# A conformer trunk: one chunk's taps moved between two projection halves, and layer norm's steps in another written order

## The chip, the cores and the metric

The kernel runs on one core of one Trainium2 chip. The metric is the device time of one execution, in microseconds. A core has five engines that run beside each other, each with a queue of its own that is worked off strictly in order: TensorE (PE, matmuls; its weight loads are listed as PEld), VectorE (DVE), ScalarE (ACT), GpSimd (POOL) and SyncE (SP), which here only starts DMAs. They wait for each other by semaphores. Matmul results land in PSUM, everything else lies in SBUF; the inputs and two small scratch tensors lie in DRAM.

## The reference

Two layers of a decoder on a sequence of 512 positions and 1024 channels. The change lies in the first one's mixer, a causal convolution module; the differential attention of the second layer, the two SwiGLU blocks and the gated embeddings are untouched.

```python
def conformer_conv(x, w_pw1, b_pw1, dw_w, dw_b, ln_g, ln_b, w_pw2, b_pw2):
    a = x @ w_pw1 + b_pw1
    u = a[..., :D_MODEL] * jax.nn.sigmoid(a[..., D_MODEL:])
    u = lax.conv_general_dilated(
        u, dw_w[:, None, :].astype(u.dtype), window_strides=(1,),
        padding=[(CONV_WIDTH - 1, 0)],
        dimension_numbers=("NWC", "WIO", "NWC"),
        feature_group_count=D_MODEL) + dw_b
    u = jax.nn.silu(layer_norm(u, ln_g, ln_b))
    return u @ w_pw2 + b_pw2

def reference(...):
    ...
    h = x
    for i in range(DEPTH):
        ...
            u = rms_norm(h, conv_norm_g[j])
            h = h + conformer_conv(u, conv_w_pw1[j], ...)
        ...
        u = rms_norm(h, ffn_norm_g[i])
        h = h + swiglu(u, ffn_w_gate[i], ffn_w_up[i], ffn_w_down[i])
        gate = jax.nn.sigmoid(rms_norm(h, ple_norm_g[i]) @ ple_w_gate[i])
        h = h + gate * (p[i] @ ple_w_proj[i])
    return h
```

The convolution has 31 taps and works on each channel alone; layer norm runs over the 1024 channels of a position.

## The kernel before

**Layout.** Activations are held transposed: eight chunks of 128 channels (on the partitions) by 512 positions. A float32 product is made of three matmuls on operands split into a rounded high part and the low rest (`mm3`, lines 165 to 169: low weight by high input, high by high, high by low). The weights are split on the chip: `weight` (line 148) loads 512 KB into `wraw`, ACT casts the high part `whi` (line 160), and VectorE subtracts it for the low part `wlo` (line 162).

**The convolution.** The loop over chunks c = 0 to 7 (line 549) makes two halves of the first projection for each chunk, gate and value, 24 matmuls each (`half`), multiplies them by the norm's row (L583, L589) and gates them (L595 or L603). The taps are spread over engines. Chunks 1, 3, 5 and 6 are "phased": all taps run on TensorE as 72 small matmuls (L457). For that, the gated chunk goes to DRAM (`pi<-big`, L420) and comes back regrouped in four pieces (`C<-pi`, L424), and nine tap matrices of 256 KB are loaded by SP (`D<-in_diag` and `C<-in_diag`, L437 to L447), four of them into buffers that the taps of an earlier phased chunk give free. The result is copied out of PSUM by ACT (L465), written to DRAM on ACT's own queue (`po<-big`, L467), read back by SP in four pieces (`B<-po`, L470), and VectorE adds bias and a shift (L475). That makes the chunk's output `y[c]`. Chunk 7, the last, is shared by three engines: VectorE makes one part as a chain of scaled additions (L505, L508), ACT and POOL a second (L495, L496), and TensorE the third, eight taps, behind all halves (L413). L512 and L514 add the three.

The table `BETWEEN` and `BEHIND` (lines 62 and 63) says behind which half of which chunk a phased chunk's taps are issued: `BETWEEN[c]` between the halves of chunk c, `BEHIND[c]` behind both. Chunk 5's taps stand behind chunk 6's halves, chunk 6's behind chunk 7's.

**Statistics.** For each finished chunk ACT makes the square (L536), and POOL adds the sum of squares and of values (L541, L543); for chunk 6 VectorE does these two. The five products of the layer's embedding factors (`factor`, `project`: six matmuls and a copy by ACT, L375) fill TensorE while chunk 7's sum is made; a sixth and two more follow later.

**Layer norm.** Behind chunk 7's sum, TensorE turns the sums into columns (L198), VectorE makes the variance in four small steps (L647, L648, L649, L259), POOL takes the power -1/2 (L261), ACT multiplies the identity by the four columns (L657), and TensorE spreads the result to a row (L660, tile `lrow`). Meanwhile TensorE makes the mean's row (L642, L643). VectorE centres chunks 0 to 2 by it (L654), POOL chunks 3 to 7 (L665). Then for each chunk: VectorE multiplies by `lrow` (L671), ACT applies Silu with gain and bias (L672) and casts the high part (L674), VectorE subtracts for the low part (L676). These are z, the input of the second projection (`linear`, line 682), whose first group makes three output chunks at a time.

**What sets the order.** The program is written in one order, and a scheduler places each engine's instructions by simulated times, except where `manual_schedule` keeps the written order on the engines named, or `issue_after` holds an instruction behind another. Buffers rotate by tag; whoever writes one waits for its last reader.

## Time and profile before

| | |
|---|---|
| median of 3 runs | 1249.22 us (1247.81 to 1250.43) |
| the profiled execution | 1246.65 us, of which the span 1244.8 us |
| mean granted clock of TensorE | 0.999 |
| chain that ended last | PE 84%, DVE 7%, issue 4%, ACT 2%, POOL 2%, DMA 1% |
| the changed stretch | about 95 to 172 us |

The span reaches from the first to the last recorded instruction. In a timeline a row gives start, duration, engine, source line, operation, output and inputs by the program's names, shape and count; in brackets stands how long the engine had been idle before it, and what ended that. A table of waits gives engine, line and releaser, with the total, the number of waits and the longest. A table of windows gives for a stretch its length, the busy time of PE, PEld, DVE, ACT and POOL with their instruction counts, the granted clock of TensorE, the busy share of the DMA engines and GB/s.

### The profile page before, as it was taken

Reading aid. Unit: us, or ns where it says so; the run is one execution under the profiler, and the core shown is the slowest. Engines: PE = TensorE matmul, PEld = TensorE weight load, DVE = VectorE, ACT = ScalarE, POOL = GpSimd, SP = SyncE. Lnnn points to the kernel's source line nnn. Section 1 sums busy time; section 2 is a strip of 40 time slices with the busy share of each in tenths; the row PEclk is TensorE's granted clock in tenths of the full one; section 3 lists DMA queues with packets and bytes.
Section 4 is the critical chain, followed back from the end, with each engine's and each line's share of the span. In section 5 each row is a group of like instructions: output and inputs, shape, how many; then the busy total and the mean of one; then the engine's idle time right before and its main releaser. Section 6 shows DMA issues by size and latency. Waiting matters only on the chain.

```text
span 1244.8 us, 18364 instructions
## 1 busy us (share of the span) xinstructions
PE 1231.8 (99%) x7048; PEld 1078.6 (87%) x7048; DVE 879.8 (71%) x1244; ACT 623.7 (50%) x1098; POOL 464.7 (37%) x351
## 2 busy tenths in 40 slices
PE   9999999999999999999999999999999999999998
PEld 7887788888998899888888888788889998999887
DVE  5997866985895479547676876646966885588535
ACT  7742464433553255435666877735434552455432
POOL 0953442024670464133436645041026650552120
PEclk9999999999999999999999999999999999999999
DMA  9756214234233322334332331142233333232331
GB/s 328 226 179 189 82 54 121 92 98 127 88 100 118 102 86 78 109 104 153 130 116 63 112 94 34 52 150 87 90 127 90 103 113 111 83 102 86 105 98 68
DMA packets 50019, 138.44 MB, mean 111 GB/s; under 512 B 5731, under 2 KB 10851, under 8 KB 49932
## 3 DMA queue, kind: packets, MB, share of 16 engines
q1 hardware_dynamic: 47664, 133.71, 34.1%
q10 hardware_dynamic: 2268, 3.57, 1.0%
q8 instruction: 55, 0.90, 0.3%
q14 instruction: 32, 0.26, 0.1%
HBM read 130.94 MB, written 6.31 MB: 110 GB/s over the span
## 4 chain that ended last, share of the span: by engine, by line
PE 84%; DVE 7%; issue 4%; ACT 2%; POOL 2%; DMA 1%; SPq 0%; DVEq 0%; POOLq 0%; ACTq 0%
PE mm L167 26%; PE mm L168 25%; PE mm L169 25%; DVE wlo L782 2%; POOL wk L496 1%; PE mm L1188 1%; DVE sc L508 1%; DVE wlo L162 1%; PE sc L457 1%; PE sc L1155 1%; PE sc L1156 1%; DVE B L873 1%; PE mm L457 1%; PE tp L1175 1%; PE tp L1109 1%
## 5 line engine op out<-in xcount | busy, mean ns | idle before, releaser
L160 ACT CAST whi<-wraw 128x1024 fp32r<-128x1024 f32 (+1 forms) x139 | 141.2, 1024 | 219.8 <-PE mm L169 110.3
L162 DVE TENSOR_TENSOR wlo<-wraw,whi 128x1024 fp32r<-128x1024 f32 (+1 forms) x135 | 174.2, 1296 | 81.9 <-ACT whi L160 81.1
L167 PE MATMUL mm<-A,wlo 128*128 128x512 f32 (+1 forms) x552 | 214.0, 388 | 0.1
L168 PE MATMUL mm<-A,whi 128*128 128x512 f32 (+1 forms) x552 | 213.4, 387 | 0.0
L169 PE MATMUL mm<-A,whi 128*128 128x512 f32 (+1 forms) x552 | 211.0, 388 | 0.0
L167 PE MATMUL mm<-B,wlo 128*128 128x512 f32 x352 | 137.0, 389 | 0.0
L168 PE MATMUL mm<-B,whi 128*128 128x512 f32 x352 | 137.0, 389 | 0.0
L169 PE MATMUL mm<-B,whi 128*128 128x512 f32 x352 | 135.6, 389 | 0.0
L228 POOL TENSOR_TENSOR acc<-acc,wk 128x512 f32<-128x512 f32 x35 | 60.3, 1724 | 189.8 <-ACT wk L227 189.2
L168 PE MATMUL mm<-C,whi 128*128 128x256 f32 x448 | 126.8, 283 | 0.0
L167 PE MATMUL mm<-C,wlo 128*128 128x256 f32 x448 | 126.8, 283 | 0.0
L169 PE MATMUL mm<-C,whi 128*128 128x256 f32 x448 | 126.8, 283 | 0.0
L169 PEld LDWEIGHTS mm<-A,whi 128*128 128x128 f32 x552 | 103.6, 188 | 22.3 <-DVE A L206 1.1
L167 PEld LDWEIGHTS mm<-A,wlo 128*128 128x128 f32 x552 | 103.8, 188 | 21.7 <-DVE h L1319 0.5
L168 PEld LDWEIGHTS mm<-A,whi 128*128 128x128 f32 x552 | 103.8, 188 | 20.5
L782 DVE TENSOR_TENSOR wlo<-A,whi 128x1024 fp32r<-128x1024 f32 x60 | 107.5, 1802 | 19.7 <-ACT whi L781 19.7
L781 ACT CAST whi<-A 128x1024 fp32r<-128x1024 f32 x60 | 62.9, 1048 | 54.6 <-PE mm L169 43.8
L791 POOL TENSOR_TENSOR A<-wraw 128x512 f32<-128x512 f32 x16 | 23.7, 1482 | 169.8 <-DMA wraw<-in_wts 147.0
L791 POOL TENSOR_TENSOR A<-A 128x512 f32<-128x512 f32 x16 | 24.6, 1536 | 165.3 <-DMA A<-in_wts 162.6
L168 PEld LDWEIGHTS mm<-C,whi 128*128 128x128 f32 x448 | 86.0, 192 | 0.2
L167 PEld LDWEIGHTS mm<-C,wlo 128*128 128x128 f32 x448 | 86.0, 192 | 0.2
L169 PEld LDWEIGHTS mm<-C,whi 128*128 128x128 f32 x448 | 86.0, 192 | 0.0
(324 smaller groups left out, 3057.1 us busy)
## 6 DMA issues: line engine op xcount, KB each, us to landing
wraw<-in_wts SPq DMA_DIRECT2D x159, 512.0 KB, 3.6
A<-in_wts SPq DMA_DIRECT2D x32, 512.0 KB, 3.6
wraw<-in_wts SPq DMA_DIRECT2D x16, 384.0 KB, 3.1
D<-in_diag SPq DMA_DIRECT2D x22, 256.0 KB, 4.5
C<-in_diag SPq DMA_DIRECT2D x16, 256.0 KB, 4.7
h<-in_xT SPq DMA_DIRECT2D x8, 256.0 KB, 4.7
B<-in_xtok SPq DMA_DIRECT2D x4, 512.0 KB, 7.2
rest<-h SPq DMA_DIRECT2D x8, 256.0 KB, 2.6
```

The costliest lines, as they stand in the source:

```text
L160: A.copy(hi[:, cut], raw[:, cut])
L162: eng.tensor_tensor(lo[:, cut], raw[:, cut], f(hi[:, cut]), ALU.subtract)
L167: T.matmul(acc, al, bh, start=first, stop=False, **kw)
L168: T.matmul(acc, ah, bh, start=False, stop=False, **kw)
L169: return T.matmul(acc, ah, bl, start=False, stop=last, **kw)
L228: self.last = self.eng.tensor_tensor(self.acc, self.acc, sq, ALU.add)
L457: last_tap[0] = T.matmul(acc[:, g * P : (g + 1) * P], w, ups[c][:, g, LEAD - m : LEAD - m + P], start=(m == 0), stop=(m == LAGS - 1),)
L496: G.tensor_tensor(pacc, pacc, pr, ALU.add)
L508: last_v_tap[0] = V.scalar_tensor_tensor(sum_, tap(j), wt(c, j), sum_, ALU.mult, ALU.add)
L781: A.copy(hi, src)
L782: V.tensor_tensor(lo, src, f(hi), ALU.subtract)
L791: G.tensor_tensor(s[:, 0], r1[:, 0], r1[:, 1], ALU.add)
```

## The change

Four things are edited.

1. Chunk 5's taps move from `BEHIND[6]` to `BETWEEN[7]`. The hold in chunk 7's chain of scaled additions behind chunk 6's shift moves from the fourth tap from the end on to the last alone.
2. The sixth factor's matmuls are written out, and its copy by ACT is written behind the four diagonal pieces.
3. Three weights of the second projection are made ahead of the variance; the third one's low part is now written ahead of the four small steps on VectorE, which are kept in that order.
4. Layer norm's steps on VectorE and ACT stand in a written order: for chunks 0 to 2, centring and product of the next chunk alternate, and a second Silu writes the high part straight from the product, in place of the cast. Chunks 3 to 7 keep Silu and cast. The first group's matmul order on chunks 0 and 1 is written out.

```diff
-BETWEEN = ((), (0,), (), (1, 2), (), (3, 4), (), ())
-BEHIND = ((), (), (), (), (), (), (5,), (6,))
+BETWEEN = ((), (0,), (), (1, 2), (), (3, 4), (), (5,))
+BEHIND = ((), (), (), (), (), (), (), (6,))
...
-            with tc.issue_after(last_shift[0].ins) if alone and j == KW - 4 else nullcontext():
+            with tc.issue_after(last_shift[0].ins) if alone and j == KW - 1 else nullcontext():
...
+        if acc is not None:
+            A.copy(o, acc)
+            pp.append(o)
+            return
...
-    factor(last_moment)
+    fifth = mm()
+    for k in range(2):
+        with tc.issue_after(last_moment[0].ins):
+            last_product[0] = mm3(fifth, wpart(pw[1], 2 + k), ph[k], k == 0, k == 1)
...
-    V.tensor_scalar(vs[:, 4:8], first_of(sums["mcols"]), 1.0 / D, None, ALU.mult)
-    V.tensor_tensor(vs[:, 4:8], vs[:, 4:8], vs[:, 4:8], ALU.mult)
-    V.scalar_tensor_tensor(vs[:, 0:4], first_of(sums["cols"]), 1.0 / D, vs[:, 4:8], ALU.mult, ALU.subtract)
-    r = rsqrt_cols(vs[:, 0:4], 4, 1.0)
-    layer_v = last_v[0]
-    with tc.issue_after(layer_v.ins):
-        for c in range(3):
-            V.scalar_tensor_tensor(y[c], sums["mean"], -1.0 / D, y[c], ALU.mult, ALU.add)
-    dg = wk()
-    for b in range(4):
-        last_dg = A.activation(dg[:, b * P : (b + 1) * P], ident, AF.Copy, scale=r[:, b : b + 1])
-    lrow = tp()
-    with tc.issue_after(last_product[0].ins):
-        last_product[0] = T.matmul(lrow, ones, dg, start=True, stop=True)
-    drow = wk()
-    with tc.issue_after(last_dg.ins):
-        A.mul(drow, sums["mean"], -1.0 / D)
-    for c in range(3, NC):
-        G.tensor_tensor(y[c], y[c], drow, ALU.add)
+    outer = [weight(after=(last_add[0], None)) for _ in range(2)]
+    raw = sb([P, 1024], "C5", 2)
+    outer.append((sb([P, 1024], "whi", 4, F32R), sb([P, 1024], "wlo", 4, F32R)))
+    nc.sync.dma_start(raw, wts[wnext[0]])
+    wnext[0] += 1
+    A.copy(outer[2][0], raw)
+    with tc.manual_schedule(engines={V.engine}):
+        V.tensor_tensor(outer[2][1], raw, f(outer[2][0]), ALU.subtract)
+        V.tensor_scalar(vs[:, 4:8], first_of(sums["mcols"]), 1.0 / D, None, ALU.mult)
+        V.tensor_tensor(vs[:, 4:8], vs[:, 4:8], vs[:, 4:8], ALU.mult)
+        V.scalar_tensor_tensor(vs[:, 0:4], first_of(sums["cols"]), 1.0 / D, vs[:, 4:8], ALU.mult, ALU.subtract)
+        r = rsqrt_cols(vs[:, 0:4], 4, 1.0)
+    dg, drow, lrow = wk(), wk(), tp()
...
+    def silu(out, c):
+        return A.activation(out, y[c], AF.Silu, scale=col("ln_g", c), bias=col("ln_b", c))
...
     with tc.manual_schedule(engines={V.engine, A.engine}):
-        for c in range(NC + 2):
-            if c < NC:
-                V.tensor_tensor(y[c], y[c], lrow, ALU.mult)
-                A.activation(y[c], y[c], AF.Silu, scale=col("ln_g", c), bias=col("ln_b", c))
+        for b in range(4):
+            A.activation(dg[:, b * P : (b + 1) * P], ident, AF.Copy, scale=r[:, b : b + 1])
+        factor(None, fifth)
+        with tc.issue_after(last_product[0].ins):
+            last_product[0] = T.matmul(lrow, ones, dg, start=True, stop=True)
+        centre(0)
+        A.mul(drow, sums["mean"], -1.0 / D)
+        for c in range(3, NC):
+            G.tensor_tensor(y[c], y[c], drow, ALU.add)
+        scaled_by_row(0)
+        for c in range(3):
+            if c < 2:
+                centre(c + 1)
+                scaled_by_row(c + 1)
+            z.append(both(sb([P, 2, S], f"A{c}", 1, F32R)))
+            silu(z[c][0], c)
+            silu(y[c], c)
+            if c < 2:
+                factor(last_product)
+            if c > 0:
+                rest(c - 1)
+        for c in range(3, NC + 1):
+            if c < NC:
+                scaled_by_row(c)
+                silu(y[c], c)
                 z.append(both(sb([P, 2, S], f"A{c}", 1, F32R)))
                 hi = A.copy(z[c][0], y[c])
-            if c >= 2:
-                lo = V.tensor_tensor(z[c - 2][1], y[c - 2], f(z[c - 2][0]), ALU.subtract)
-            if c < 2:
-                factor(last_product)
+            lo = rest(c - 1)
             if c == 3:
                 third = lo, hi
```

`centre`, `scaled_by_row` and `rest` are the three VectorE steps of before (centring, product, low part), each as a function of the chunk.

TensorE, where chunk 7's gate half and chunk 5's taps meet. Names: `mm_1085` (before) and `mm_1022` (now) are the gate half of chunk 7, `mm_1110` and `mm_1100` its value half, `sc` is chunk 5's tap sum. Before:

```order
L169 MATMUL mm_978<-A_40_172,whi_749 128x512
L167 MATMUL mm_1085<-A_33_141,wlo_943 128x512
L168 MATMUL mm_1085<-A_33_141,whi_942 128x512
L169 MATMUL mm_1085<-A_33_141,whi_942 128x512
L167 MATMUL mm_1085<-A_34_146,wlo_943 128x512
L168 MATMUL mm_1085<-A_34_146,whi_942 128x512
L457 MATMUL sc_1003<-C_162_867,D_187_1004 128x128 x4
```

And of the change:

```order
L167 MATMUL mm_1022<-A_40_172,wlo_943 128x512
L168 MATMUL mm_1022<-A_40_172,whi_942 128x512
L169 MATMUL mm_1022<-A_40_172,whi_942 128x512
L457 MATMUL sc_1047<-C_162_867,D_193_1048 128x128 x4
L457 MATMUL sc_1047<-C_162_867,D_194_1050 128x128 x4
```

Before, the taps stood behind five of the gate half's 24 matmuls; now they stand behind all 24.

ACT between chunk 7's halves and the tap products. `big<-sc` with the DMA `po` is chunk 5's way out, `wk_1223` chunk 5's square, `whi_1453` (before) and `whi_1367` (now) the high part of a later weight, whose buffer chunk 7's value half frees. Before:

```order
L160 CAST whi_1218<-wraw_1217 128x1024
L465 COPY big_1071<-sc_1003 128x512
L467 DMA po_1073<-big_1071 128x512
L536 ACTIVATE wk_1207<-B_176_915 128x512
L160 CAST whi_1447<-wraw_1446 128x1024
L584 ACTIVATE big_1188<-big_1188,vec_63 128x512
```

And of the change:

```order
L536 ACTIVATE wk_1207<-B_176_915 128x512
L160 CAST whi_1367<-wraw_1366 128x1024
L465 COPY big_1187<-sc_1047 128x512
L495 ACTIVATE C_238_1287<-C_211_1184,C_31_133 128x512
L467 DMA po_1189<-big_1187 128x512
L495 ACTIVATE C_239_1290<-C_211_1184,C_31_133 128x512
L495 ACTIVATE C_240_1293<-C_211_1184,C_31_133 128x512
L495 ACTIVATE C_241_1296<-C_211_1184,C_31_133 128x512
L536 ACTIVATE wk_1223<-B_213_1191 128x512
L465 COPY big_1197<-mm_1125 128x512
```

Chunk 5's copy and DMA now stand behind the cast and the first tap product, and chunk 5's square stands ahead of chunk 6's copy. On VectorE chunk 5's shift (L475) moves accordingly from ahead of chunk 7's gating to behind the sixth step of chunk 7's chain, and chunk 6's shift from four steps ahead of its end to two. On SP chunk 6's regrouped input now leaves ahead of all of its first four tap matrices, and chunk 5's return behind both matrices of chunk 7.

VectorE from the end of the convolution into layer norm. `B_244` is chunk 7's output, `v` the variance's columns, `B_82`, `B_117`, `B_129` chunks 0 to 2, `A` the low parts of z. Before:

```order
L514 TENSOR_TENSOR B_244_1305<-mm_1227,B_244_1305 128x512
L162 TENSOR_TENSOR wlo_1448<-wraw_1446,whi_1447 128x1024
L162 TENSOR_TENSOR wlo_1454<-wraw_1452,whi_1453 128x1024
L647 TENSOR_SCALAR v_253_1361<-sc_1333 128x4
L648 TENSOR_TENSOR v_253_1361<-v_253_1361 128x4
L649 SCALAR_TENSOR_TENSOR v_253_1361<-tp_1331,v_253_1361 128x4
L259 TENSOR_SCALAR v_254_1365<-v_253_1361 128x4
L162 TENSOR_TENSOR wlo_1460<-C_276_1458,whi_1459 128x1024
L654 SCALAR_TENSOR_TENSOR B_82_376<-tp_1332,B_82_376 128x512
L654 SCALAR_TENSOR_TENSOR B_117_609<-tp_1332,B_117_609 128x512
```

And of the change:

```order
L162 TENSOR_TENSOR wlo_1368<-wraw_1366,whi_1367 128x1024
L661 TENSOR_TENSOR wlo_1374<-C_259_1372,whi_1373 128x1024
L662 TENSOR_SCALAR v_252_1359<-sc_1333 128x4
L663 TENSOR_TENSOR v_252_1359<-v_252_1359 128x4
L664 SCALAR_TENSOR_TENSOR v_252_1359<-tp_1331,v_252_1359 128x4
L259 TENSOR_SCALAR v_262_1383<-v_252_1359 128x4
L669 SCALAR_TENSOR_TENSOR B_82_376<-tp_1332,B_82_376 128x512
L672 TENSOR_TENSOR B_82_376<-B_82_376,tp_1390 128x512
L669 SCALAR_TENSOR_TENSOR B_117_609<-tp_1332,B_117_609 128x512
L672 TENSOR_TENSOR B_117_609<-B_117_609,tp_1390 128x512
L669 SCALAR_TENSOR_TENSOR B_129_647<-tp_1332,B_129_647 128x512
L680 TENSOR_TENSOR A_268_1410<-B_82_376,A_268_1410 128x512
```

The third weight's low part moved from behind the variance's steps to ahead of them. Two of the three centrings moved behind a product with the row `tp_1390`, and the first low part of z behind all three products.

More of the change, by code (lines that the diff above doesn't have):

```diff
@@ L612, in trunk, with factor @@
     pw = [weight(), weight()]
-    def factor(after):
+    def factor(after, acc=None):
         m = len(pp)
@@ L655, in trunk @@
-    dg = wk()
-    for b in range(4):
-        last_dg = A.activation(dg[:, b * P : (b + 1) * P], ident, AF.Copy, scale=r[:, b : b + 1])
-    lrow = tp()
-    with tc.issue_after(last_product[0].ins):
-        last_product[0] = T.matmul(lrow, ones, dg, start=True, stop=True)
-    drow = wk()
-    with tc.issue_after(last_dg.ins):
-        A.mul(drow, sums["mean"], -1.0 / D)
-    for c in range(3, NC):
-        G.tensor_tensor(y[c], y[c], drow, ALU.add)
-    z = []
-    with tc.manual_schedule(engines={V.engine, A.engine}):
-        for c in range(NC + 2):
+    outer = [weight(after=(last_add[0], None)) for _ in range(2)]
@@ new lines, in trunk, with centre, scaled_by_row, rest @@
+    dg, drow, lrow = wk(), wk(), tp()
+    def centre(c):
+        V.scalar_tensor_tensor(y[c], sums["mean"], -1.0 / D, y[c], ALU.mult, ALU.add)
+    def scaled_by_row(c):
+        V.tensor_tensor(y[c], y[c], lrow, ALU.mult)
+    def silu(out, c):
+        return A.activation(out, y[c], AF.Silu, scale=col("ln_g", c), bias=col("ln_b", c))
+    z = []
+    def rest(c):
+        return V.tensor_tensor(z[c][1], y[c], f(z[c][0]), ALU.subtract)
+    with tc.manual_schedule(engines={V.engine, A.engine}):
+        for b in range(4):
[8 more added lines that the diff above has]
+        scaled_by_row(0)
+        for c in range(3):
+            if c < 2:
[9 more added lines that the diff above has]
+        for c in range(3, NC + 1):
@@ L698, in linear @@
                     before(k)
+                if g == 3 and k < 2:
+                    (bh, bl), parts = src[k], [wpart(w_, k) for w_ in ws]
+                    for (ah, al), a_ in zip(parts, accs):
+                        T.matmul(a_, al, bh, start=k == 0, stop=False)
+                        T.matmul(a_, ah, bh, start=False, stop=False)
+                    for (ah, al), a_ in zip(parts, accs):
+                        T.matmul(a_, ah, bl, start=False, stop=False)
+                    continue
                 for w_, a_ in zip(ws, accs):
@@ L711, in add_conv @@
         norm.chunk(m)
-    linear(NC, z, add_conv, 3, split={0: (last_add[0], None), 1: (last_add[0], None), 2: (layer_v, None), 3: third}, home=("C5", 2))
+    linear(NC, z, add_conv, 3, split={3: third}, given=dict(enumerate(outer)))
     def tops(tag):
```

## The prediction

> **What bounds the kernel now.** I read the page's busy times first, then TensorE's waits, then the timeline of each engine between 95 and 170 us, where all edits lie.
>
> ```profile
> PE 1231.8 (99%) x7048; PEld 1078.6 (87%) x7048; DVE 879.8 (71%) x1244; ACT 623.7 (50%) x1098; POOL 464.7 (37%) x351
> PE sc L457 <- DMA C<-pi: 3.0, 1, 3.0
> PE sc L1155 <- DVE st L1158: 1.3, 2, 1.0
> PE tp L660 <- ACT wk L657: 0.7, 1, 0.7
> ```
>
> TensorE is busy for 99% of the span: time can only be won where it stands still or runs slowly. Its largest wait (total, times, longest) is one of 3.0 us for `C<-pi`, the regrouped input of chunk 5's taps. The 0.7 us at line 660 is layer norm's row of factors. Both are in the changed stretch. TensorE's timeline:
>
> ```profile
> 100.66 0.39 PE L167 MATMUL mm<-A,wlo 128*128 128x512 f32 x1
> 101.56 0.39 PE L168 MATMUL mm<-A,whi 128*128 128x512 f32 x1
> 104.90 5.81 PE L457 MATMUL sc<-C,D 128*128 128x128 f32 x36 [2.95 <-DMA C<-pi]
> 114.49 0.48 PE L169 MATMUL mm<-A,whi 128*128 128x512 f32 x1
> 124.35 4.18 PE L457 MATMUL mm<-C,D 128*128 128x128 f32 x36
> 132.38 7.04 PE L413 MATMUL mm<-C,D 128*128 128x512 f32 x16
> ...
> 104.90:108.20 3.30, 3.30 (x15) 3.30 (x16) 2.97 (x4) 1.57 (x2) 1.75 (x2) 0.51 0.42 150
> ```
>
> Chunk 7's gate half starts at 100.66; five of its 24 matmuls run, then the taps hold the queue until 104.90. They run slowly too: 104.90 to 114.49 is 9.59 us, chunk 6's same 72 matmuls take 124.35 to 132.38, 8.03 us. The last row, of the table by windows, says why: granted clock 0.51 (third number from its end) for 3.3 us after the gap.
>
> **Chunk 5's taps.** The other 19 gate matmuls, at (101.56 - 100.66) / 4 = 0.225 us each, go ahead and fill 101.79 to 106.1. The input was there at 104.90, so nothing waits and the clock stays. Saved on TensorE: 104.90 - 101.79 = 3.11 of standing, and 9.59 - 8.03 = 1.56 of half clock, **4.67 us**. Chunk 7's second half then ends at 124.35 - 4.67 = 119.68.
>
> SP's queue changes with it. Chunk 6's first four tap matrices, three of which left before its `C<-pi` did, now all stand behind it, and chunk 5's return stands behind chunk 7's two matrices, the second of which waits for a buffer that chunk 6's first taps free (about 121, early enough). The four leave by about 115.6 (chunk 6's input goes out from 112.11 for 1.75 us as before, by SP's row below, then 0.44 each) and have 4 us until 119.68; the page's median to landing is 4.5 us (row `D<-in_diag` below), so up to 0.5 us of standing, which the idle time found below covers; without that cover it would cost those 0.5. I cost it at nothing.
>
> **VectorE and the way back from DRAM.** This is the second chain to the same point, the last convolution chunk's sum (L514).
>
> ```profile
> 126.15 1.12 DVE L475 SCALAR_TENSOR_TENSOR B<-B,vec,shrow 128x512 f32<-128x512 f32 x1 [6.35 <-DMA B<-po]
> 127.19 0.68 DVE L589 TENSOR_TENSOR big<-mm,rb 128x512 f32<-128x512 f32 x1
> 127.97 1.27 DVE L603 SCALAR_TENSOR_TENSOR C<-big,vec,big 128x512 f32<-128x512 f32 x1
> 130.97 8.67 DVE L508 SCALAR_TENSOR_TENSOR sc<-C,C,sc 128x512 f32<-128x512 f32 x11
> 139.68 1.85 DVE L475 SCALAR_TENSOR_TENSOR B<-B,vec,shrow 128x512 f32<-128x512 f32 x1
> 146.46 0.69 DVE L514 TENSOR_TENSOR B<-mm,B 128x512 f32<-128x512 f32 x1
> ...
> 118.58 0.33 ACTq L467 DMA_DIRECT2D po<-big  x1
> 127.36 0.63 ACT L536 ACTIVATE wk<-B 128x512 f32<-128x512 f32 x1 [4.69 <-DVE B L475]
> 132.59 0.59 ACT L465 COPY big<-mm 128x512 f32<-128x512 f32 x1 [0.74 <-PE mm L457]
> 133.20 0.33 ACTq L467 DMA_DIRECT2D po<-big  x1
> ...
> 112.11 1.75 SPq L424 DMA_DIRECT2D C<-pi  x4
> 122.68 1.75 SPq L470 DMA_DIRECT2D B<-po  x4
> 135.19 1.75 SPq L470 DMA_DIRECT2D B<-po  x4
> ...
> D<-in_diag SPq DMA_DIRECT2D x22, 256.0 KB, 4.5
> ...
> 133.96 8.67 POOL L496 TENSOR_TENSOR wk<-wk,C 128x512 f32<-128x512 f32 x6 [3.58 <-ACT wk L492]
> ...
> 114.50:122.50 8.00, 8.00 (x38) 6.65 (x37) 4.83 (x7) 4.10 (x6) 2.55 (x2) 1.00 1.04 294
> 132.50:139.50 7.00, 7.00 (x19) 3.12 (x18) 6.68 (x10) 2.74 (x4) 5.23 (x5) 1.00 0.35 121
> ```
>
> Now L589 starts at about 119.9, L603 at 120.7 (+0.78), ending at 121.95. Chunk 5's copy-out and its DMA now stand on ACT behind a split that waits for chunk 7's second half, and the DMA behind a tap product that waits for L603: it leaves at 122.0 instead of 118.58. From there to the return's issue took 4.10 us with the DMA engines full (share 1.04) and 1.99 with them at 0.35. The matrices drain by about 122, so I take 2.4, near the quiet row. From the return to L475 it is 3.47 for chunk 5 and at most 4.49 for chunk 6, where VectorE came last; I take 3.6. Chunk 5's L475 starts at **128.0**, bounds 127.5 and 130.6.
>
> VectorE goes on at 129.05 and does eight products at 8.67 / 11 = 0.79: 135.35. On ACT, chunk 5's square (0.63) now stands ahead of chunk 6's copy-out (0.59), both behind L475's end at 129.1: DMA at 130.3, + 1.99 + 3.47 = 135.8 for chunk 6's L475 (up to 136.8). So 0.45 us of waiting, 1.8 for L475 beside POOL (1.85, less what the next overlaps), two products 1.6: 139.2. POOL first does chunk 5's two sums (to 131.7), then its six products, 8.67 us, to 140.4: L543 and L541 run partly beside it, 0.69 each when alone (L514's row), up to 1.2 beside it (the low parts below), so L512 at 141.0 and, 0.78 behind it, L514 at **141.75**, 4.7 us earlier. This keeps pace with TensorE, with no slack.
>
> **The third low part, ahead of the variance.** Row 150.13 below was free, because it lay under POOL's power. Now it stands in front.
>
> ```profile
> 148.20 1.22 DVE L162 TENSOR_TENSOR wlo<-wraw,whi 128x1024 fp32r<-128x1024 f32 x1
> 149.34 0.15 DVE L647 TENSOR_SCALAR v<-sc 128x4 f32<-128x4 f32 x1
> 149.85 0.16 DVE L649 SCALAR_TENSOR_TENSOR v<-tp,v 128x4 f32<-128x4 f32 x1 [0.16 <-PE tp L198]
> 150.13 1.23 DVE L162 TENSOR_TENSOR wlo<-C,whi 128x1024 fp32r<-128x1024 f32 x1
> ...
> 150.30 1.94 POOL L261 TENSOR_TENSOR r<-v,mhalf 128x4 f32<-128x4 f32 x1 [7.67 <-DVE v L259]
> ...
> 153.60 1.12 PE L660 MATMUL tp<-wk,ones 128*128 128x512 f32 x2 [0.69 <-ACT wk L657]
> ```
>
> From L514 to L647 it was 149.34 - 146.46 = 2.88; with the third part 1.14 more (148.20 to 149.34): 145.75. The four small steps took 0.96 with 0.16 of waiting, so 0.80, and the power starts at 146.55. TensorE's sums would allow 150.30 - 4.67 = 145.63. VectorE is last now, and the power, ACT's four diagonal pieces and L660 move by 150.30 - 146.55 = **3.75 us**, not 4.67. TensorE's own work before L660 ends 4.67 earlier, so its wait grows from 0.69 to about 1.6 us.
>
> **Centring, products, Silu.** From L660's end on:
>
> ```profile
> 154.76 1.88 DVE L671 TENSOR_TENSOR B<-B,tp 128x512 f32<-128x512 f32 x3
> 156.99 1.72 DVE L676 TENSOR_TENSOR A<-B,A 128x512 fp32r<-128x512 f32 x1 [0.34 <-ACT A L674]
> 159.23 1.18 DVE L676 TENSOR_TENSOR A<-B,A 128x512 fp32r<-128x512 f32 x1
> ...
> 155.49 0.82 ACT L672 ACTIVATE B<-B,vec 128x512 f32<-128x512 f32 x1
> 156.33 0.62 ACT L674 CAST A<-B 128x512 fp32r<-128x512 f32 x1
> ...
> 158.76 0.97 PE L169 MATMUL mm<-A,whi 128*128 128x512 f32 x3
> ```
>
> Before, three centrings were done when the row came (154.72); now only the first is. VectorE does product, centring, product, centring, product and only then the first low part of z: 0.60 for a step that doesn't need the one ahead, 0.78 for one that does (as L589 to L603), 3.36 in all, so it starts 3.4 us behind the row, not 2.27. It takes 1.18 to 1.72 beside POOL's five centrings and is done at 4.6 to 5.1; TensorE wants it at 158.76 - 154.72 = 4.04. That gives back 0.55 to 1.1; I take **0.85**. The high parts aren't what TensorE waits for: before, the first was cast at 156.95, 2.2 behind the row, and TensorE took it some 1.4 us ahead of L169, at 2.6; now a Silu writes it at about 1.6. A Silu in place of a cast costs ACT 0.82 - 0.62 = 0.2 us, three times, and VectorE's low parts come after them anyway. The fifth projection's copy moves behind the diagonal pieces and nothing waits for it; the explicit matmul order is what stood there before.
>
> **Sum.** -4.67 of standing and slow clock, + 0.92 by which VectorE lags, + 0.85 at the first low part: **-2.9 us**. Behind it the order is the same and TensorE is the bound, so it should last to the end. The profiled execution took 1246.65 us (span 1244.8), so 1243.75; it lay 2.6 below the median 1249.22, and on the median's scale I predict **1246.3**.
>
> **The rivals.**
> 1. VectorE keeps up: the return at the quiet price throughout, the first low part hardly late. -4.67 + 0.1 to 0.9, about -4, **1245.2**. For it: DMA share 0.35 behind 132. Against: no slack in the chain. 0.14.
> 2. The clock falls in the longer wait at L660: the same 1.56 us again, -2.9 + 1.56 = -1.3, **1247.9**. The rows show a fall after 2.95 us and none after 1.0 or 0.7; 1.6 lies between. The Trainium skill, "TensorE: Matmul & The Clock Gate", section "Part 1: The HAM clock gate", lets the clock fall only after an idle window of some 3.4 us that runs free. By that rule the sum stays at -2.9; the trace doesn't agree on the size, since 2.95 us was enough, and the row decides. 0.15.
> 3. Chunk 5's way back costs what it can cost by the busy rows, 4.10 + 4.49: L475 at 130.6, chunk 6's by its upper bound too, 2.6 to 3.6 later than forecast in all. L660 goes with it, TensorE stands there for 4.2 us or more, and the clock falls: -2.9 + 3.1 + 1.56 = +1.8, **1251.0**. 0.09.
> 4. Slower: both ways back at the busy prices. Chunk 6's L475 is then 5.7 us late, L660 comes 2.0 later than before, and the clock falls: +2.0 + 0.85 + 1.56 = +4.4, **1253.6**. The place is the row of factors, and it decides once L660 gains less than 2.4 us (0.85 + 1.56). For it: ACT's queue, which puts chunk 5's DMA behind chunk 7's half. Against it and 3: the heavy loads are over by 122. 0.10.
>
> **How the numbers follow.** 0.52 for the forecast, 0.14, 0.15, 0.09 and 0.10 for the rivals. 0.2% is 2.5 us, about what a measurement of this kernel can tell from no change; the forecast lies just past it, so I give 0.35 of its chance to faster. Faster 0.35 + 0.14 = 0.49; same 0.17 + 0.15 + 0.09 = 0.41; slower 0.10. The range takes in the forecast, rivals 1 and 2 and a run's scatter of some 1.2 us (1247.81 to 1250.43), and reaches to rival 3: 1243.5 to 1250.6.
>
> **What would show it.** Right: the wait for `C<-pi` gone and clock 1.00 at 104 to 109; chunk 5's taps in 8.0 us; chunk 5's L475 near 128; L514 4.7 earlier, the power only 3.75; a wait of about 1.6 us for the factors' row, and one of under 1 us for the first low part of z. Wrong: a wait at chunk 6's taps, L475 beyond 130, a clock below 1 around 150, or a new wait behind 170.

## The result, and the profile after

| | before | changed kernel |
|---|---|---|
| median, range | 1248.43 us (1246.50 to 1250.71) | 1245.37 us (1242.85 to 1247.22) |
| ratio, 95% interval | | 0.9972 (0.9962 to 0.9982) |
| span of the profiled execution | 1244.8 us | 1241.9 us |

The change gains 0.28% by the ratio, some 3.5 us on this scale; the medians differ by 3.1 and the two spans by 2.9. A later measurement of the same kernel gave 0.9970 (0.9960 to 0.9980). Forecast were 1246.3 us, the range held, and the sum was -2.9. But several terms of that sum were off and cancelled, as the rows show. TensorE's timeline in the changed kernel, with its waits in brackets, and a row of the table by windows:

```profile
106.20 4.18 PE L457 MATMUL sc<-C,D 128*128 128x128 f32 x36
114.15 0.48 PE L167 MATMUL mm<-A,wlo 128*128 128x512 f32 x1
121.11 4.54 PE L457 MATMUL mm<-C,D 128*128 128x128 f32 x36 [1.26 <-DMA D<-in_diag]
151.03 1.12 PE L687 MATMUL tp<-wk,ones 128*128 128x512 f32 x2 [0.99 <-ACT wk L684]
156.44 0.96 PE L737 MATMUL mm<-A,whi 128*128 128x512 f32 x3 [0.18 <-DVE A L680]
...
104.90:108.20 3.30, 3.30 (x25) 3.07 (x24) 2.44 (x3) 1.30 (x2) 1.19 (x1) 1.00 0.53 153
```

The 3.0 us for `C<-pi` are gone: nothing is waited for at 106.20. In their place stand 1.26 us for chunk 6's matrices; the wait for the row of factors (now line 687) has gone from 0.69 to 0.99. Chunk 5's taps take 114.15 - 106.20 = 7.95 us where they took 9.59, at a clock of 1.00, and chunk 7's second half ends at 121.11 - 1.26 = 119.85. VectorE, the DMA issues of ScalarE (ACTq) and SyncE (SPq), and POOL, from their timelines:

```profile
129.44 1.11 DVE L475 SCALAR_TENSOR_TENSOR B<-B,vec,shrow 128x512 f32<-128x512 f32 x1 [1.93 <-DMA B<-po]
137.87 1.51 DVE L475 SCALAR_TENSOR_TENSOR B<-B,vec,shrow 128x512 f32<-128x512 f32 x1 [1.12 <-DMA B<-po]
140.75 1.67 DVE L543 TENSOR_TENSOR acc<-acc,B 128x512 f32<-128x512 f32 x1
143.73 0.69 DVE L514 TENSOR_TENSOR B<-mm,B 128x512 f32<-128x512 f32 x1
155.45 0.94 DVE L680 TENSOR_TENSOR A<-B,A 128x512 fp32r<-128x512 f32 x1
...
122.05 0.33 ACTq L467 DMA_DIRECT2D po<-big  x1
...
112.66 2.86 SPq L424 DMA_DIRECT2D C<-pi  x4
126.18 1.75 SPq L470 DMA_DIRECT2D B<-po  x4
...
133.15 8.72 POOL L496 TENSOR_TENSOR wk<-wk,C 128x512 f32<-128x512 f32 x6
148.65 1.02 POOL L261 TENSOR_TENSOR r<-v,mhalf 128x4 f32<-128x4 f32 x1 [6.78 <-DVE v L259]
```

VectorE waits for the way back of both chunks (1.93 and 1.12 us). Behind chunk 5's L475 POOL makes that chunk's two sums and then its six products for chunk 7, from 130.70 to 133.15 + 8.72 = 141.87 without a pause. VectorE's L543 stands beside the last of them (1.67 us, 0.68 before), and L514 comes 1.86 behind their end. So here L514 hangs on chunk 5's way back, by way of POOL. The last convolution sum (L514) comes at 143.73, 2.73 us sooner than before, not 4.7. POOL's power takes 1.02 us, not 1.94: that gives 0.92 back where the prediction had nothing. So the row of factors moves by 153.60 - 151.03 = 2.57 and the first low part's product (156.44, before 158.76) by 2.32. Behind layer norm the distance between the two traces wanders between 1.8 and 2.9 us, and is 2.9 at the end.

### The profile page after: what moved, and what is told of

Same layout as the page of the kernel before. It is cut to its first block, busy times and chain, and to the rows that moved or that the text cites. A ratio compares the mean times of both kernels' runs of the same rounds, so it can differ in the third digit from the quotient of the medians.

```text
span 1241.9 us, 18364 instructions
## 1 busy us (share of the span) xinstructions
PE 1230.2 (99%) x7048; PEld 1077.1 (87%) x7048; DVE 878.7 (71%) x1244; ACT 624.8 (50%) x1098; POOL 464.9 (37%) x351
## 3 DMA queue, kind: packets, MB, share of 16 engines
q10 hardware_dynamic: 2268, 3.57, 1.0%
## 4 chain that ended last, share of the span: by engine, by line
PE 84%; DVE 7%; DMA 3%; issue 3%; ACT 2%; POOL 2%; SPq 0%; ACTq 0%; DVEq 0%; POOLq 0%
PE mm L167 26%; PE mm L168 26%; PE mm L169 26%; DVE sc L508 2%; POOL wk L496 2%; DMA wraw<-in_wts 1%; DVE wlo L162 1%; PE mm L1228 1%; DMA B<-po 1%; PE sc L1195 1%; PE sc L1196 1%; PE tp L1215 1%; PE tp L1149 1%; DMA po<-big 0%; DVE wlo L822 0%
## 5 line engine op out<-in xcount | busy, mean ns | idle before, releaser
L168 PE MATMUL mm<-A,whi 128*128 128x512 f32 (+1 forms) x546 | 211.1, 387 | 0.0
L169 PE MATMUL mm<-A,whi 128*128 128x512 f32 (+1 forms) x546 | 208.9, 387 | 0.1
L822 DVE TENSOR_TENSOR wlo<-A,whi 128x1024 fp32r<-128x1024 f32 x60 | 104.9, 1758 | 20.4 <-ACT whi L821 20.4
```

The costliest lines, as they stand in the source:

```text
L168: T.matmul(acc, ah, bh, start=False, stop=False, **kw)
L169: return T.matmul(acc, ah, bl, start=False, stop=last, **kw)
L822: V.tensor_tensor(lo, src, f(hi), ALU.subtract)
```

## The experiments

There were twelve runs, in three groups of four, each group beside the kernel before (1248.4 to 1248.5 us in each). All times are medians and all ratios are against that kernel. Waits for DMA vary from one execution to the next, and the profiles lie up to 2 us apart ahead of everything that is edited (chunk 2's sum, L512, starts between 90.72 and 93.05), so stages are compared by distances inside one trace where that can be done. "The way back" is the road of a phased chunk's result: copy out of PSUM, transfer to DRAM (`po`), four loads back on SyncE, L475.

**The taps alone.** The kernel before with the first part of the change.

```diff
-BETWEEN = ((), (0,), (), (1, 2), (), (3, 4), (), ())
-BEHIND = ((), (), (), (), (), (), (5,), (6,))
+BETWEEN = ((), (0,), (), (1, 2), (), (3, 4), (), (5,))
+BEHIND = ((), (), (), (), (), (), (), (6,))
...
-            with tc.issue_after(last_shift[0].ins) if alone and j == KW - 4 else nullcontext():
+            with tc.issue_after(last_shift[0].ins) if alone and j == KW - 1 else nullcontext():
```

> The kernel before with the first part of the change alone: chunk 5's taps between the last pair's halves and VectorE's last tap of chunk 7 in place of the fourth-last; layer norm as it was. Theory A (the whole gain is the taps' and ends at the last VectorE addition of chunk 7; the layer-norm edits cancel out): TensorE and VectorE up to that addition as in the changed kernel, the addition 2.7 us earlier than before; POOL's power again long (1.9 us, beside the third low part) but its input ready about 0.9 us sooner than in the changed kernel, so the row of factors and all behind it about 2.9 us earlier than before: 1245.5 us, ratio 0.9977. Theory B (the layer-norm edits bring a gain of their own): 1.0 us or more of the 2.9 missing, 1246.6 us or more.

Measured: 1244.47 us, ratio 0.9966 (0.9954 to 0.9977): all of the gain. Its timelines:

```profile
145.75 0.69 DVE L514 TENSOR_TENSOR B<-mm,B 128x512 f32<-128x512 f32 x1
149.37 1.23 DVE L162 TENSOR_TENSOR wlo<-C,whi 128x1024 fp32r<-128x1024 f32 x1
...
149.54 1.94 POOL L261 TENSOR_TENSOR r<-v,mhalf 128x4 f32<-128x4 f32 x1 [5.64 <-DVE v L259]
...
152.84 1.13 PE L660 MATMUL tp<-wk,ones 128*128 128x512 f32 x2 [1.19 <-ACT wk L657]
157.91 0.84 PE L169 MATMUL mm<-A,whi 128*128 128x512 f32 x3
```

The power is long again. From L514 to the first low part's product it takes 157.91 - 145.75 = 12.16 us; in the changed kernel 156.44 - 143.73 = 12.71. Layer norm's edits lose about half a microsecond there. What I had expected of L514, 2.7 us sooner than before, this profile doesn't show: it is 0.71 sooner, and the span is 0.7 shorter. The profiled execution (1245.90 us) was among the slower of the ten, VectorE was 93.05 - 91.18 = 1.87 us behind the changed kernel's already at chunk 2's sum (L512), and TensorE waited 0.99 us for `C<-pi`. So that the whole gain is here is read from the medians alone.

**Layer norm alone.** The kernel before with the other edits; the taps stay behind both halves. The diff is that of the change without the three lines above.

> The kernel before with the layer-norm edits alone (the third low part ahead of the variance, the centring and products in the other order, the second Silu, the copy of the fifth projection behind); chunk 5's taps stay behind both halves. Theory A: the power's input about 1.0 us later, the power 0.9 us shorter, the first low part 0.2 us later, so 0.0 to +0.5 us against before: 1248.4 to 1248.9 us, no change that can be told. Theory B: the edits bring a gain of their own, 1.0 us or more, 1247.4 us or less. My prediction's terms (the third low part +1.14 and the order of the products +0.85, nothing back from the power) would make it +2.0 us, 1250.4 us.

Measured: 1248.98 us, ratio 1.0005 (0.9996 to 1.0014). Its rows:

```profile
149.06 0.69 DVE L514 TENSOR_TENSOR B<-mm,B 128x512 f32<-128x512 f32 x1
...
153.98 1.02 POOL L261 TENSOR_TENSOR r<-v,mhalf 128x4 f32<-128x4 f32 x1 [8.76 <-DVE v L259]
...
106.55 6.76 PE L457 MATMUL sc<-C,D 128*128 128x128 f32 x36 [4.33 <-DMA C<-pi]
156.37 1.12 PE L687 MATMUL tp<-wk,ones 128*128 128x512 f32 x2 [0.86 <-ACT wk L684]
161.78 0.97 PE L737 MATMUL mm<-A,whi 128*128 128x512 f32 x3 [0.19 <-DVE A L680]
```

161.78 - 149.06 = 12.72 us from L514 to the first low part's product; before it was 158.76 - 146.46 = 12.30. So the edits cost 0.4 us here, as theory A has it, and neither a gain of 1 us nor the loss of 2 us by my terms is there. The wait for `C<-pi` was 4.33 us in this execution, 2.95 in that of before, though nothing ahead of it is edited: it differs from one execution to the next.

**The third low part behind the variance again.** In the changed kernel:

```diff
     with tc.manual_schedule(engines={V.engine}):
-        V.tensor_tensor(outer[2][1], raw, f(outer[2][0]), ALU.subtract)
...
         r = rsqrt_cols(vs[:, 0:4], 4, 1.0)
+        V.tensor_tensor(outer[2][1], raw, f(outer[2][0]), ALU.subtract)
```

> The changed kernel with the third low part moved back behind the variance on VectorE, beside POOL's power. Theory A (a subtraction with two operands in SBUF beside the power stretches it from 1.02 to 1.94 us, so the move is worth only about 0.2 us): the power's input 1.1 to 1.2 us earlier, the power 1.9 us, the row of factors 0.2 us earlier, 1245.2 us, not to be told from the changed kernel. Theory B (that place was free, as the prediction had it): the power stays 1.02 us, the row and the end 1.1 us earlier, 1244.3 us.

Measured: 1245.23 us, ratio 0.9974 (0.9966 to 0.9983). Its rows:

```profile
143.96 0.69 DVE L514 TENSOR_TENSOR B<-mm,B 128x512 f32<-128x512 f32 x1
147.58 1.23 DVE L665 TENSOR_TENSOR wlo<-C,whi 128x1024 fp32r<-128x1024 f32 x1
...
147.75 1.94 POOL L261 TENSOR_TENSOR r<-v,mhalf 128x4 f32<-128x4 f32 x1 [6.03 <-DVE v L259]
...
151.05 1.12 PE L687 MATMUL tp<-wk,ones 128*128 128x512 f32 x2 [1.19 <-ACT wk L684]
```

The power starts 147.75 - 143.96 = 3.79 us behind L514 instead of 148.65 - 143.73 = 4.92, but takes 0.92 longer: the row of factors comes 7.09 behind L514 instead of 7.30. Theory A has it to the tenth: 0.2 us. The times can't tell this. The subtraction ends at 147.58 + 1.23 = 148.81, and the power at 149.69, 0.88 later; in the run with the taps alone 150.60 and 151.48, 0.88 as well, and before 151.36 and 152.24, again 0.88. In all three the power starts 0.17 us behind the subtraction, so the equal 0.88 alone could also be a power that runs slowly. POOL's sum L541 in the kernel before, with another length and another distance, tells the two apart:

```profile
120.28 1.29 POOL L541 TENSOR_TENSOR B<-B,wk 128x512 f32<-128x512 f32 x1
128.65 1.74 POOL L541 TENSOR_TENSOR B<-B,wk 128x512 f32<-128x512 f32 x1
```

VectorE idles beside the first. The second starts 0.68 us behind VectorE's L603 (127.97 to 129.24, two inputs in SBUF) and ends at 130.39, 1.15 behind that one's end. Both POOL instructions end behind VectorE's end by what they take alone less 0.14: 1.02 - 0.88 and 1.29 - 1.15. So the power does not run slowly beside the subtraction: it stands until that is over, and then takes a little less than alone. The Trainium skill, "SBUF — State Buffer", section "SBUF: two separate sides", says that VectorE with two SBUF inputs and GpSimd lock one pair of ports for a whole instruction and that the one that comes second is blocked entirely; three traces agree, with the same 0.88.

**Chunk 5's copy and transfer first.** ScalarE had idled ahead of the square of y4, which stood ahead of chunk 5's copy. In the changed kernel (`outs[c]` is the transfer to DRAM):

```diff
-        with tc.issue_after(last_factor[0].ins) if c > NC - 3 else nullcontext():
+        behind = last_factor[0] if c > NC - 3 else outs[5] if c == NC - 4 else None
+        with tc.issue_after(behind.ins) if behind else nullcontext():
             A.activation(sq, y[c], AF.Square)
...
-    outer = [weight(after=(last_add[0], None)) for _ in range(2)]
+    outer = [weight(after=(last_add[0], None)), weight(after=(last_add[0], outs[5]))]
```

> The changed kernel with chunk 5's copy out of PSUM and its transfer to DRAM ahead of the square of y4 and of a weight's cast on ScalarE, where ScalarE idled for 3.2 us. Theory A (the way back of chunk 5 is what held VectorE: a wait of 1.93 us for it, and 1.12 us for chunk 6's, in the changed kernel): the transfer leaves 3 to 5 us sooner, at 117 to 119 us; the first wait goes and most of it comes back at chunk 6, whose copy still stands behind chunk 5's square; the last addition of chunk 7 comes 0.5 to 2.0 us sooner and the row of factors up to 1.2 us sooner (TensorE's sums are then the last): 1244.2 to 1245.4 us. Theory B (VectorE's chain is covered by something else, as TensorE's later taps of chunk 6): chunk 7's last addition sooner, the row of factors unmoved, 1245.4 us.

Measured: 1243.72 us, ratio 0.9965 (0.9953 to 0.9977). Its rows:

```profile
119.49 0.33 ACTq L467 DMA_DIRECT2D po<-big  x1
125.71 1.75 SPq L470 DMA_DIRECT2D B<-po  x4
129.00 1.10 DVE L475 SCALAR_TENSOR_TENSOR B<-B,vec,shrow 128x512 f32<-128x512 f32 x1 [1.99 <-DMA B<-po]
```

The transfer left 2.6 us sooner and came back 0.5 us sooner: 6.22 us from issue to issue instead of 4.13. Theory A failed on this, since the wait on VectorE stayed (1.99 us): what holds the way back is not when it starts.

**Chunk 6's copy first, too.** The run above with one more square behind a transfer:

```diff
-        behind = last_factor[0] if c > NC - 3 else outs[5] if c == NC - 4 else None
+        behind = last_factor[0] if c > NC - 3 else outs[c + 1] if c > NC - 5 else None
```

> As the run with chunk 5's copy ahead of the square of y4, and chunk 6's copy and transfer also ahead of the square of y5. In that run the earlier transfer landed hardly sooner: it waited behind the matrices of chunks 6 and 7 in the queues. Theory A (two transfers in two different states: chunk 5's is held by the traffic, chunk 6's by ScalarE's square of y5, which waits for VectorE): chunk 6's transfer leaves when its taps end, 0.5 to 1.2 us sooner, its VectorE row and chunk 7's last addition follow by as much as VectorE's taps allow (at most 0.7 us, its wait there); the row of factors at most 0.5 us sooner than in that run: 1243.2 to 1243.8 us. Theory B (VectorE is no longer what ends last): no change from that run, 1243.7 us.

Measured: 1244.46 us, ratio 0.9965 (0.9953 to 0.9977). Nothing more came of it, as theory B has it, though by time (1242.6 to 1245.6 us, from the interval) both theories stand. In its trace VectorE no longer waits for chunk 6's way back, but L514 stands 143.91 - 129.62 = 14.29 us behind chunk 5's L475, as in the run before it (143.26 - 129.00 = 14.26) and in the changed kernel (14.29): POOL's sums and products fill that time, and chunk 6's way back was not what held it.

**Chunk 6's matrices from ScalarE's queue.** In the changed kernel:

```diff
-                    nc.sync.dma_start(two[m], diag[i + 2 * g + m])
+                    by_act.append((nc.scalar if c == NC - 2 else nc.sync).dma_start(two[m], diag[i + 2 * g + m]))
...
-        gated = A.activation(tg, tg, AF.Sigmoid, bias=col("b_pw1", 8 + c))
+        with ExitStack() as held:
+            for i in by_act[-4:] if c == NC - 1 else ():
+                held.enter_context(tc.issue_after(i.ins))
+            gated = A.activation(tg, tg, AF.Sigmoid, bias=col("b_pw1", 8 + c))
```

> The changed kernel with the first four loads of chunk 6's matrices issued from ScalarE's queue ahead of the last gate (ScalarE idles there for 5 us) in place of SyncE's, where they stand behind the wait for chunk 6's own rows. Theory A (TensorE's wait for them, 1.3 us and 0.4 us of slower taps, is covered by VectorE's wait for chunk 5's way back): the loads leave 4 to 5 us sooner, TensorE's wait for them goes, down to what the PSUM buffer allows (0.3 to 0.6 us, freed by the sum of y4); but because the queues are also less full when chunk 5's transfer leaves, that lands up to 1.5 us sooner, and the end moves by 0.3 to 1.0 us: 1244.4 to 1245.1 us. Theory B (the matrices' wait is what the end hangs on): the end moves by the whole 1.3 us or more, 1244.1 us or less, whatever chunk 5's transfer does. Theory C (covered, and the traffic is no matter): no change, 1245.4 us.

Measured: 1243.80 us, ratio 0.9963 (0.9951 to 0.9975). Its rows, with one of the table by windows (granted clock, DMA share and GB/s at the end):

```profile
107.39 0.34 ACTq L437 DMA_DIRECT2D D<-in_diag  x1
112.66 3.62 ACTq L437 DMA_DIRECT2D D<-in_diag  x2
...
119.43 4.18 PE L457 MATMUL mm<-C,D 128*128 128x128 f32 x36
149.39 1.12 PE L690 MATMUL tp<-wk,ones 128*128 128x512 f32 x2 [1.41 <-ACT wk L687]
...
122.02 0.33 ACTq L467 DMA_DIRECT2D po<-big  x1
124.53 1.75 SPq L470 DMA_DIRECT2D B<-po  x4
127.79 1.11 DVE L475 SCALAR_TENSOR_TENSOR B<-B,vec,shrow 128x512 f32<-128x512 f32 x1 [0.29 <-DMA B<-po]
142.09 0.69 DVE L514 TENSOR_TENSOR B<-mm,B 128x512 f32<-128x512 f32 x1
131.50 8.73 POOL L496 TENSOR_TENSOR wk<-wk,C 128x512 f32<-128x512 f32 x6
...
122.00:126.20 4.20, 4.20 (x40) 4.20 (x39) 4.06 (x5) 2.50 (x4) 0.98 (x1) 1.00 0.44 165
```

SyncE's row and the same window in the changed kernel:

```profile
115.61 2.35 SPq L437 DMA_DIRECT2D D<-in_diag  x4
...
122.00:126.20 4.20, 4.18 (x38) 3.99 (x37) 4.06 (x5) 2.53 (x4) 1.00 (x1) 1.00 0.86 318
```

This settles the way back. Chunk 5's transfer leaves at the same time as in the changed kernel (122.02 and 122.05), but four loads of 256 KB have left from 107.39 on (two by 107.92, two from 112.66) instead of from 115.61, the DMA engines carry 165 GB/s in that window instead of 318, and it takes 124.53 - 122.02 = 2.51 us instead of 4.13. The other profiles with the transfer at this place agree: 4.31, 3.83 and 3.57 with the loads on SyncE's queue (changed kernel again, taps alone, third low part behind), 3.01 with them on ScalarE's and layer norm as before. L475 is at 127.79, where I had forecast 128.0, and L514 at 142.09 (forecast 141.75). TensorE's wait for the matrices is gone, wholly. The row of factors comes 151.03 - 149.39 = 1.64 us sooner, more than theory A had and about what theory B had. Which chain brought that, the rows tell. L514 is 143.73 - 142.09 = 1.64 sooner as well, and the row stands 7.30 behind L514 in both kernels. L514 again stands 142.09 - 127.79 = 14.30 behind chunk 5's L475, and 1.86 behind the end of POOL's products (131.50 + 8.73). So the gain came by chunk 5's way back, the mechanism of theory A; the time that TensorE won at the matrices only made its wait for the row longer, 1.41 instead of 0.99. By time (1242.4 to 1245.4 us, from the interval) all three theories stand.

**Chunk 7's matrices behind chunk 5's way back**, with both copies first:

```diff
-                with after_weights(c):
+                with tc.issue_after(back[5].ins) if c == NC - 1 else after_weights(c):
                     nc.sync.dma_start(dg[:, :n], diag[TAPS.index((c, j)), :, :n])
```

> Both copies out first, and the two loads of chunk 7's matrices behind chunk 5's four loads back on SyncE's queue. Theory A (the way back of chunk 5 takes 6 us to land since some 10 loads of matrices of 256 KB each, at 350 to 400 GB/s, are in the queues with it, and its way in waits behind chunk 7's two loads on SyncE): with those two behind, the transfer lands 1 to 1.5 us sooner and the wait on VectorE for it (1.99 us) falls to 0.5 to 1.0; chunk 7's last addition 1 us sooner than with both out first alone, the row of factors then set by TensorE's sums: 0.3 to 0.6 us sooner, 1243.2 us. Chunk 7's matrices are still there when its taps begin. Theory B (the landing does not hang on those two): no change, or slower by up to 1 us if chunk 7's taps now wait for their matrices.

Measured: 1243.81 us, ratio 0.9964 (0.9950 to 0.9977). Its rows, and its largest wait on TensorE:

```profile
120.23 0.33 ACTq L467 DMA_DIRECT2D po<-big  x1
126.25 1.75 SPq L470 DMA_DIRECT2D B<-po  x4
...
PE mm L457 <- DMA C<-in_diag: 2.5, 1, 2.5
```

6.02 us on the way, and TensorE waits 2.5 us for chunk 6's matrices. Theory B: without chunk 7's two loads ahead of it the transfer takes as long as in the run with chunk 5's copy first (6.22), so they were not what it stood with; the run before this one says that it was chunk 6's loads. Whether the early transfer delays those in turn isn't shown, since the wait for them varies in the changed kernel as well (below).

**All three together**, run in two groups:

> All three together: both copies out first, chunk 7's matrices behind chunk 5's way back, and chunk 6's matrices from ScalarE's queue. Theory A: VectorE's two waits and TensorE's wait for the matrices all shrink; TensorE's chain up to the sums is then 0.7 to 1.3 us shorter than in the changed kernel, VectorE's 2 us, and the row of factors follows TensorE: 1.0 to 2.0 us faster than the changed kernel, 1243.4 to 1244.4 us. Theory B (the DMA queues set the stage, whatever the order): no more than the best of the others, 1243.7 us.

> The three moves together (both copies out first, chunk 7's matrices behind chunk 5's way back, chunk 6's matrices from ScalarE's queue) once more, beside the changed kernel. Theory A (the way back's price was the queue of chunk 6's matrices, and with it gone TensorE is the last ahead of the row of factors): 1.0 to 2.0 us under the changed kernel of the same call. Theory B (what is gained ahead of layer norm is given back later): within 0.5 us of it.

Measured: 1243.22 us, ratio 0.9958 (0.9946 to 0.9970), and 1243.15 us, ratio 0.9964 (0.9952 to 0.9977). In the second group the changed kernel ran beside it:

> The changed kernel unaltered, once more, on the same chip as the three runs beside it, to set them against it. All theories: 1245.4 us, ratio 0.9972; its wait on VectorE for chunk 5's way back again between 1.4 and 2.0 us and TensorE's wait for chunk 6's matrices up to 1.3 us.

Measured: 1243.97 us, ratio 0.9970 (0.9960 to 0.9980). The difference is 0.8 us, between the two theories and inside the intervals. The waits of the two profiles in that group, first the changed kernel's:

```profile
PE mm L457 <- DMA C<-in_diag: 2.9, 1, 2.9
PE sc L457 <- DMA C<-pi: 0.9, 1, 0.9
```

and with all three moves:

```profile
PE mm L413 <- DVE B L475: 0.8, 1, 0.8
```

So the wait for chunk 6's matrices differs from one execution of the changed kernel to the next: 1.3 us in the first profile, 2.9 in this one, where I had expected up to 1.3. With the loads on ScalarE's queue it did not appear in any of five profiles; with the taps' part and the loads on SyncE's queue five of seven show it (0.9 to 2.9 us). Nor did theory A hold whole: in both profiles with all three moves VectorE's wait for chunk 5 is gone, but that for chunk 6 is 1.6 and 1.7 us, where it was 1.1 and 1.7 in the changed kernel.

**The taps' part with chunk 6's matrices moved, and with all three moves; layer norm as before.**

> The kernel before with the taps' part of the change and chunk 6's first four loads from ScalarE's queue, layer norm as it was. Theory A (the layer-norm edits cost 0.2 to 0.5 us from chunk 7's last addition to the first low part; the loads are worth 1.0 to 1.6 us): 0.3 to 0.5 us under the run of the changed kernel with those loads moved, 1243.4 us. Theory B (with VectorE early, the third low part beside POOL's power costs its 0.9 us in full, so the change's layer norm is the better): 1244.2 us or more.

> The kernel before with the taps' part of the change and all three moves, layer norm as it was. Theory A: 0.3 to 0.5 us under the same with the changed layer norm (the run beside it), 1242.8 us. Theory B (as for the run before this one): the same or up to 0.5 us over it.

Measured: 1243.12 us, ratio 0.9961 (0.9948 to 0.9973), and 1243.98 us, ratio 0.9970 (0.9959 to 0.9981). The first is 0.7 us under its counterpart with the changed layer norm (1243.80, in another group), the second 0.8 us over its own (1243.15). In the second TensorE waits 1.3 us for chunk 7's matrices, which stand behind chunk 5's way back there; its counterpart doesn't show this wait, so that pair compares more than the two layer norms. Which layer norm is the better one can't be settled with these intervals. No version here is shown to be faster than the changed kernel. The five with chunk 6's loads on ScalarE's queue lie at 1243.12 to 1243.98; those with the taps' part and without that move at 1243.72 to 1245.37: about 1 us between the means, suggestive and no more.

## Why the prediction was right, point by point

| step | predicted | measured |
|---|---|---|
| chunk 7's second half ends | 119.68 | 119.85 |
| wait for chunk 6's matrices | 0 (up to 0.5) | 1.26, and 4.54 - 4.18 = 0.36 more inside the taps |
| transfer to return's issue, chunk 5 | 2.4 | 126.18 - 122.05 = 4.13 |
| chunk 5's L475 | 128.0 | 129.44 |
| chunk 6's L475 | 135.8 | 137.87 |
| POOL's six products end | 140.4 | 141.87 |
| L514 against before | -4.7 | -2.73 |
| power starts | 146.55 | 148.65 |
| length of the power against before | 0 | -0.92 |
| row of factors against before | -3.75 | -2.57 |
| wait for that row | 1.6 | 0.99 |
| first low part's delay | 0.85 | 0.25 |
| sum | -2.9 | -2.9 |

**Chunk 5's taps** were right in mechanism and size: no wait, no half clock, 7.95 us. The medians of the run with the taps alone show that the gain is theirs. That nothing waits holds for this execution and not for each: 0.9 us of the wait for `C<-pi` are back in the second profile of the changed kernel, and 1.0 with the taps alone.

**Chunk 6's matrices** were right in kind and mis-sized. It was the issue that I had wrong: all four were to be gone by 115.6, and they left from 115.61 on, in 2.35 us, because SyncE took 2.86 us for the four regrouped pieces ahead of them instead of 1.75. Their landing took 3.7 us (median of the four), less than the 4.5 that I had taken. That the wait was covered by TensorE's later idle time, as I wrote, the rows bear out: TensorE still waits 0.99 us at the row of factors, and with the loads moved the row follows L514 by the same 7.30.

**The way back of chunk 5** is the step that failed: "The matrices drain by about 122, so I take 2.4, near the quiet row." In the part on the taps I had found that these matrices now leave behind `C<-pi`, so late that TensorE nearly waits for them, and did not carry that to the DMA engines: the same delay moves the traffic under the transfer. The busy row of before, 4.10 us, was the right price (4.13), and with the four loads out of the way it fell to 2.51. Chunk 5's L475 came 1.44 us late by it, POOL's products with it, and this is the most of the 2 us that L514 lacks. The rest, 0.5, lies between POOL's products and L514, 1.86 us instead of the 1.35 of my sum: I had VectorE's two sums of chunk 6 run partly beside the products, and L543 stood until the last of these was over. My upper bound of 130.6 held.

**The third low part:** "Row 150.13 below was free, because it lay under POOL's power" was wrong. It lengthened the power that it lay under. The same power elsewhere in the kernel before, on POOL's timeline, would have told:

```profile
211.24 1.02 POOL L261 TENSOR_TENSOR r<-v,mhalf 128x4 f32<-128x4 f32 x1 [4.43 <-DVE v L259]
```

Its 1.14 us ahead of the variance was right, but 0.92 come back: 0.2 net.

**The first low part** was mis-sized: my range for the subtraction beside POOL began at 1.18 us, it took 0.94, and TensorE waited 0.18 us.

**The rivals.** The clock did not fall at the row of factors: the wait was only 0.99, and where it was 1.41, with the loads on ScalarE's queue, the clock stayed at 1.00 too. The busy price of rivals 3 and 4 did come, for chunk 5's transfer alone (from its return to L475 it took 129.44 - 126.18 = 3.26, not 4.49), and cost less than they had it, since chunk 6's L475 came at 137.87 instead of 138.4 to 139.4 and the power was shorter. What I lost with the way back (2.0 us at L514), I got back with the power (0.9) and with the low part (0.6); the last 0.6, between -2.3 there and -2.9 at the end, came behind layer norm, where the order is the same, and isn't explained by the change: by POOL's powers the distance between the two traces is 2.33 at 208.91 and at 557.87, 1.80 at 608.72 and 2.91 at 1202.42. The sum was right partly by luck.

## What to carry to other kernels

When a change delays a burst of loads, move the burst on the time axis and price every small transfer that now falls under it at the busy rate, also those on other queues. When an instruction seems free because it lies beside a short one of another engine, look at that one's length elsewhere in the same trace: POOL's power took 1.02 us there, and 1.94 here. And when a sum comes out right, compare its terms, not only its total.

## What the runs showed of the hardware

The clock of TensorE. Before, TensorE stood still for 2.95 us and the clock fell; in the second profile of the changed kernel it stood still for 2.93 us at 120.66 and the clock stayed. The table by windows, before:

```profile
101.34:104.75 3.41, 0.61 (x3) 0.19 (x1) 2.72 (x4) 0.72 (x1) 0.00 (x0) 1.00 0.68 164
104.75:108.16 3.41, 3.26 (x15) 3.29 (x16) 2.93 (x4) 1.57 (x2) 1.71 (x2) 0.50 0.54 155
108.16:111.58 3.42, 3.42 (x33) 3.42 (x32) 3.42 (x5) 0.00 (x0) 0.80 (x1) 1.00 0.43 150
```

The clock was 0.50 for exactly one piece of 3.41 us, and the piece ahead of it held 0.61 us of work. In the run with layer norm alone, where the wait was 4.33 us, it was 0.50 for two such pieces:

```profile
104.99:108.40 3.41, 1.85 (x9) 1.88 (x10) 1.55 (x2) 0.42 (x1) 0.31 (x1) 0.50 0.67 184
108.40:111.81 3.41, 3.41 (x18) 3.41 (x17) 3.38 (x6) 1.15 (x2) 2.19 (x2) 0.50 0.31 77
```

This looks like a judgement over pieces of 3.41 us that do not start with the wait: a wait of 2.9 us makes the clock fall when it lies nearly whole in one piece, and not when it is cut in two. Where the pieces lay in the second profile of the changed kernel can be worked out, if they run on without a break. Before, the clock rises at 108.16 and falls at the end, at 1244.80; at 3.41 to 3.42 us each these 1136.64 us can only be 333 whole pieces, of 3.4133. In the second profile the clock falls at the end at 1244.69, and 329 such pieces ahead of that is 121.70, within the wait (120.66 to 123.59):

```profile
121.71:125.12 3.41, 1.53 (x14) 1.56 (x15) 3.23 (x4) 3.41 (x6) 2.71 (x2) 1.00 1.02 376
```

So the wait was cut in two, the piece from 118.29 on held 2.37 us of work and this one 1.53, and the clock stayed at 1.00 in both. The Trainium skill, "TensorE: Matmul & The Clock Gate", section "Part 1: The HAM clock gate", describes such a free-running window, of 3413 ns; the rows agree, and add that a window with 0.61 us of work in it was idle enough and one with 1.53 was not. In the prediction I had read the Trainium skill as speaking against the row (2.95 us being less than 3.4); with a window that need not be wholly idle the two agree.

GpSimd beside VectorE. POOL's power took 1.02 us alone, and 1.94 in each of the five kernels in which a VectorE subtraction with two inputs in SBUF starts 0.17 us ahead of it; it stood still until that one's end. VectorE stands in the same way beside POOL: L543 took 1.67 us beside POOL's last product, and ended 0.55 behind it, where alone it takes 0.68.
